# Spreading the top-16 steps and gate writes of a PEER layer, with an early norm, a bias spread in DRAM and a new tail

## The chip, the cores and the metric

The kernel runs on one core of a Trainium2 chip. The metric is the device time of one execution in microseconds (us), the median over runs. A core has five engines that run their instruction streams in order and side by side: TensorE (PE, matmul, with its weight load as PEld), VectorE (DVE), ScalarE (ACT), GpSimd (POOL) and SyncE (SP). SP issues most DMAs, POOL the others. Sixteen DMA engines move the data of all queues.

## The reference

One layer of a decoder with batch 1, 256 tokens (T) and width 2048 (D), all in fp32:

```python
h = h + concat(nsa(rmsnorm(h)), stick_breaking(rmsnorm(h))) @ w_out
h = h + memory_attention(rmsnorm(h), rmsnorm(mem))
h = h + peer_ffn(rmsnorm(h))
return rmsnorm(h, norm_final)
```

The change touches three places of it. In the NSA attention a T5 bias, which depends only on the distance of query and key, is added to the logits of 8 heads. In PEER each of 8 heads projects a token to two queries of 128, scores each against 128 sub-keys, takes the 16 best of both, then the 16 best of their 256 sums, and so chooses 16 of 16384 experts:

```python
q = (xt @ w_pq).reshape(T, 8, 2, 128)
s = jnp.einsum('thpd,hpkd->thpk', q, sub_keys)
top_s, top_i = lax.top_k(s, 16)
cand = top_s[:, :, 0, :, None] + top_s[:, :, 1, None, :]
best_s, best_c = lax.top_k(cand.reshape(T, 8, 256), 16)
expert = ia * 128 + ib                     # of the two winners
gate = jax.nn.softmax(best_s, axis=-1)
a = jnp.einsum('td,ted->te', xb, u_tab[eb])
out = jnp.einsum('te,ted->td', gate * jax.nn.gelu(a), v_tab[eb])
```

The last place is the closing rmsnorm over the 256 x 2048 result.

## The kernel before

Every fp32 weight tile of 128 x 1024 ("raw", 512 KB, loaded by SP) is split for TensorE: ACT copies it to `hi` (L72), DVE forms the rest `lo` = raw - hi (L74). `fm_block` multiplies two such halves: per half eight matmuls of `hi` with the pair of the activations' high and low parts (L109) and eight of `lo` with the high part (L111). `join` adds the two parts of the result (ACT L144, DVE L145). There are 4 buffers of raw and 3 each of hi and lo.

The stages in order: attention over memory and tokens with its projections, up to about 547 us, of which `bias_table` prepares the T5 bias; PEER's queries, 16 blocks of `w_pq` (8 heads h, two queries p2 each); 128 blocks of U (`u_chunk`), one for each 128 experts, which hold for all tokens the gelu of their dot products; then V.

The block h = 7, p2 = 1 is `whole_block`: raw fp32 matmuls (L138) with `whole`, the unsplit activations. `whole` is put together on POOL from the two parts of `x3` (L712). After it `renew` multiplies `whole` by the tokens' `rstd` (L795, in place) and splits it anew into `x3` (L796, L797) for the U blocks, which so work on normed tokens; the `w_pq` blocks before work on tokens without `rstd`, which `keys` puts into the scores (L934).

The top-16 is cut into 48 pieces: for each head and half of the tokens (tb) `keys` (scores on PE L932, 16 best of each side), `pairs` (best 16 of 256 sums, softmax) and a third (`ids` and `sums`: expert numbers, `place` as a table index, and for experts that an earlier head chose too, the sum of the gates with `dup`, L989 to L995, growing with the head). Nearly all of it is DVE work on 16 to 256 (at the end 1792) elements a partition. `topk_pieces` returns the three functions, the loop calls one a block.

A gate goes to a table in DRAM by `put_gate` (L1016): an indirect DMA on POOL writing 128 words of 4 bytes, 256 of them (128 for each tb). `some` issues the next few, each `behind` a recent `lo` (a wait on the last or last but one `lo` issued, so POOL goes in step with the blocks). Later the table is read back (L810), multiplied with the gelu values, the hit tokens of each expert are counted and listed (`lists`), rows are written (L904) and V rows are fetched (L1067). In the V phase `run(0)` to `run(3)` go over lists of experts by halves; `steps` are functions that it calls between the halves, one every second turn; `closing` then forms the final rmsnorm for both halves of the tokens from the eight accumulators in PSUM, and stores it.

The program's order on each engine is set by a scheduler that simulates the program and honours data dependencies, buffers and added dependencies (`add_manual_dep`). `SYNC` as its kind is a wait on the chip; the change adds a kind `NoSync`, which only fixes an order within an engine.

Of the kernel before, what the change touches and what calls it, by code (L numbers as in the profile page):

```python
# [22 lines left out]
SYNC = mybir.DependencyInfo(mybir.DependencyClass.Sync, mybir.DependencyReason.DATA)  # L23
AF = mybir.ActivationFunctionType
# [3 lines left out]
T = 256  # L28
# [24 lines left out]
class Layer:  # L53
    def __init__(self, tc, a):
        self.tc, self.nc, self.a = tc, tc.nc, a
        self.written = ([], [])
        self.spread = {}
        self.pace = []

# [9 lines left out]
    def parts(self, raw, eng=None):  # L69
# [5 lines left out]
        self.pace.append(self.last_lo)  # L75
        return hi, lo
# [20 lines left out]
    def scaled(self, raw, val):  # L97
# [4 lines left out]
        self.last_lo = nc.vector.scalar_tensor_tensor(lo, raw, val, hi.bitcast(F32), op0=ALU.mult, op1=ALU.subtract)  # L102
        return hi, lo

# [75 lines left out]
    def rsqrt(self, v, y, tmp):  # L180
# [7 lines left out]
        nc.vector.tensor_mul(y, y, tmp)  # L188
# [53 lines left out]
    def front(self):  # L242
        nc, tc, a = self.nc, self.tc, self.a
        with ExitStack() as es:
# [52 lines left out]
            turned = self.bias_table()  # L297
# [23 lines left out]
            turned()  # L321
# [113 lines left out]
    def bias_table(self):  # L435
# [10 lines left out]
        row = fp.tile([8, 512], F32, tag="p", name="row", bufs=2)  # L446
        nc.vector.tensor_add(row, p, neg)

        dr = self.dram.tile([8, 512], F32, name="bias_rows")
        nc.gpsimd.dma_start(dr, row)  # L450
# [4 lines left out]
        turn = fp.tile([128, 128], F32, tag="tri", name="turn")  # L455
        nc.gpsimd.dma_start(turn, a["turn"])
# [4 lines left out]
        def turned():  # L461
            for tb in range(2):
                for h in range(0, 8, 2):
                    p = self.ps.tile([128, 2, T], F32, tag="lg", name="ps_turn", bufs=2)
                    nc.tensor.matmul(p, turn, rev[:, tb, h:h + 2, :], start=True, stop=True)
                    nc.scalar.activation(self.bias[:, tb, h:h + 2, :], p, AF.Copy)

        return turned
# [202 lines left out]
    def peer(self):  # L671
        nc, tc, a = self.nc, self.tc, self.a
        with ExitStack() as es:
# [13 lines left out]
            def some(todo=puts, n=3):  # L687

                if not n:
                    n = 3 + beat[0] % 2  # L690
                    beat[0] += 1
# [4 lines left out]
            with ExitStack() as e2:  # L696
                ps = self.ps = e2.enter_context(tc.tile_pool(name="ups", bufs=2, reuse_waits="tile", space=bass.MemoryType.PSUM))
                pieces = []
                with tc.tile_pool(name="tk", bufs=1, reuse_waits="tile") as tk:
                    self.tk = tk  # L700
                    self.gate = [tk.tile([128, 128], F32, name="gate%d" % tb) for tb in range(2)]
                    self.spot = [tk.tile([128, 128], F32, name="spot%d" % tb) for tb in range(2)]
# [6 lines left out]
                    for q in range(4):  # L709
                        xs = slice(q * 4, q * 4 + 4)  # L710
                        x32 = self.x3[:, xs, :].bitcast(F32)
                        nc.gpsimd.tensor_add(whole[:, xs, :], x32[:, :, :T], x32[:, :, T:])  # L712
                    for h in range(8):
                        sk = tk.tile([128, 2, 128], F32, tag="sk", name="sk", bufs=2)
# [5 lines left out]
                        for p2 in range(2):  # L720
                            q = tk.tile([128, T], F32, tag="q", name="q", bufs=4)
# [30 lines left out]
                end = c + (len(puts) + 2) // 3  # L752
# [5 lines left out]
                while c < 128:  # L758
# [8 lines left out]
                    self.u_chunk(c, c >= first)  # L767
                    for g, t in done.pop(c, []):
# [3 lines left out]
                    some()  # L772
# [11 lines left out]
                    if not steps:  # L784
                        some(late)
# [4 lines left out]
    def renew(self, whole):  # L790
        nc = self.nc
        for q in range(4):
            xs = slice(q * 4, q * 4 + 4)
            src = whole[:, xs, :]
            nc.vector.tensor_tensor(out=src, in0=src, in1=self.rstd.unsqueeze(1).to_broadcast([128, 4, T]), op=ALU.mult)  # L795
# [610 lines left out]
```

## Time and profile before

| | |
|---|---|
| median of 3 runs | 1749.74 us (1748.86 to 1755.26) |
| profiled execution | 1753.41 us |
| its span, first to last instruction | 1751.4 us |
| mean granted TensorE clock | 0.977 |
| PE busy | 1656.6 us, 95% |
| DVE busy | 1248.1 us, 71% |
| ACT busy | 984.6 us, 56% |
| POOL busy | 743.7 us, 42% |
| DMA | 414.93 MB, mean 237 GB/s |

The page of the profile divides the span into 40 equal slices and gives the busy share of each engine in tenths, and the clock that TensorE was granted. Other views give busy times by stretches of time, groups of instructions by line and operation ("xcount | busy us, mean ns | idle time before, and what ended it"), waits ("engine line waited for: us in total, times, longest"), and the chain of work that ended last, followed back from the end. "remote" or "another core or an unknown queue" there stands for a semaphore whose writer the profile doesn't show. Matmuls overlap, so their mean durations add up to more than the busy time.

### The profile page before, as it was taken

To read this page: it belongs to the slowest core of one execution; us is meant where nothing else is said; L and a number is where in the kernel's file an instruction comes from. 1 tells how busy PE (TensorE), PEld (TensorE's weight loads), DVE (VectorE), ACT (ScalarE), POOL (GpSimd) and SP (SyncE) were. 2 spreads that over 40 slices of the span, in tenths; PEclk is the share of its full clock that TensorE was granted. 3 is DMA by queue.
4 is the path that set the end of the run, shared out by engine and by line. 5 is a ranking of instruction groups with operands and counts; after the bars stand their busy time and mean duration, and the time that the engine had idled before them with its cause. 6 is when DMAs were issued, how large, how long until landed. Compare 5 with 4: busy or idle time off the path is not lost.

```text
span 1751.4 us, 25883 instructions
## 1 busy us (share of the span) xinstructions
PE 1656.6 (95%) x8864; PEld 1400.7 (80%) x8864; DVE 1248.1 (71%) x2231; ACT 984.6 (56%) x1457; POOL 743.7 (42%) x652
## 2 busy tenths in 40 slices
PE   8999999999999786999999999999999988999996
PEld 6788777888888675888888888888888776777885
DVE  6835475556659789999994557886666568788687
ACT  6534556765565333665654446664555446666566
POOL 5510000112217444787886551103655307786620
PEclk9999999999999888999999999999999999999998
DMA  8656435789946543565666657886888965998991
GB/s 295 228 171 209 143 104 193 275 318 362 333 143 189 173 124 104 175 193 173 199 193 176 189 180 258 283 281 220 262 258 262 351 252 202 415 385 332 412 399 61
DMA packets 136475, 414.93 MB, mean 237 GB/s; under 512 B 39177, under 2 KB 52105, under 8 KB 122768
## 3 DMA queue, kind: packets, MB, share of 16 engines
q1 hardware_dynamic: 97712, 254.21, 45.4%
q0 software_dynamic: 38624, 158.99, 24.0%
q8 instruction: 71, 1.16, 0.3%
q14 instruction: 68, 0.56, 0.1%
HBM read 369.26 MB, written 49.65 MB: 239 GB/s over the span
## 4 chain that ended last, share of the span: by engine, by line
PE 54%; DVE 7%; DMA 5%; issue 4%; ACT 2%; POOL 1%; another core or an unknown queue 1%; POOLq 0%; ACTq 0%; DVEq 0%
PE acc L109 28%; PE acc L111 14%; PE out L1095 11%; DMA raw<-U 2%; DVE lo L74 2%; DMA vrows<-V,index 1%; ACT hi L72 1%; DVE pair_f L177 1%; DMA gates<-table 1%; POOL rows L904 1%; DMA rows<-hb,where 1%; POOL vrows L1067 0%; PE out L1197 0%; PE ps_s L932 0%
## 5 line engine op out<-in xcount | busy, mean ns | idle before, releaser
L74 DVE TENSOR_TENSOR lo<-raw,hi 128x1024 fp32r<-128x1024 f32 x433 | 535.4, 1240 | 303.8 <-ACT hi L72 210.7
L72 ACT ACTIVATE hi<-raw 128x1024 fp32r<-128x1024 f32 x437 | 461.1, 1058 | 452.5 <-issue 161.3
L109 PE MATMUL acc<-pair_f,hi 128*128 128x512 f32 x2288 | 580.8, 396 | 17.2 <-ACT hi L72 7.4
L109 PEld LDWEIGHTS acc<-pair_f,hi 128*128 128x128 f32 x2288 | 415.9, 191 | 96.4 <-ACT hi L72 8.3
L1016 POOL DMA_INDIRECT table<-total,place x256 | 308.6, 1206 | 177.3 <-DVE lo L74 69.6
L111 PEld LDWEIGHTS acc<-pair_f,lo 128*128 128x128 f32 x2288 | 314.1, 192 | 23.6 <-DVE lo L74 1.6
L111 PE MATMUL acc<-pair_f,lo 128*128 128x256 f32 x2288 | 322.3, 284 | 1.4 <-issue 0.8
L904 POOL DMA_INDIRECT rows<-hb,where x128 | 153.8, 1201 | 123.3 <-DVE lo L74 76.2
L102 DVE SCALAR_TENSOR_TENSOR lo<-vrows,val,hi 128x1024 fp32r<-128x1024 f32 x96 | 122.7, 1284 | 42.4 <-ACT hi L100 33.2
L100 ACT ACTIVATE hi<-vrows,val 128x1024 fp32r<-128x1024 f32 x96 | 109.0, 1147 | 78.1 <-PE out L1095 36.2
L1067 POOL DMA_INDIRECT vrows<-V,index x88 | 116.6, 1325 | 65.4 <-issue 19.2
L109 PE MATMUL acc<-pair_x,hi 128*128 128x512 f32 x512 | 131.9, 396 | 0.0
L74 DVE TENSOR_TENSOR lo<-vrows,hi 128x1024 fp32r<-128x1024 f32 x80 | 97.8, 1223 | 16.0 <-ACT hi L72 6.6
L109 PEld LDWEIGHTS acc<-pair_x,hi 128*128 128x128 f32 x512 | 91.7, 189 | 17.2 <-issue 1.4
L72 ACT ACTIVATE hi<-vrows 128x1024 fp32r<-128x1024 f32 x80 | 84.2, 1052 | 26.5 <-PE out L1095 20.9
L1095 PE MATMUL out<-hi,hh 128*128 128x512 f32 x256 | 79.7, 405 | 4.5 <-DVE ut L145 2.3
L1095 PE MATMUL out<-hi,hl 128*128 128x512 f32 x256 | 81.5, 403 | 1.0 <-DVE hl L1104 0.4
L1095 PE MATMUL out<-lo,hh 128*128 128x512 f32 x256 | 76.7, 402 | 0.2 <-DVE lo L74 0.2
L111 PEld LDWEIGHTS acc<-pair_x,lo 128*128 128x128 f32 x512 | 71.1, 192 | 5.2
L111 PE MATMUL acc<-pair_x,lo 128*128 128x256 f32 x512 | 75.1, 286 | 0.0
L109 PE MATMUL acc<-pair_o,hi 128*128 128x512 f32 x256 | 65.0, 394 | 5.7 <-ACT hi L72 4.7
L1095 PE MATMUL out<-hi,listed 128*128 128x512 f32 x192 | 59.7, 402 | 5.0 <-ACT hi L100 4.5
(393 smaller groups left out, 2209.4 us busy)
## 6 DMA issues: line engine op xcount, KB each, us to landing
raw<-U SPq DMA_DIRECT2D x256, 512.0 KB
raw<-w_sb SPq DMA_DIRECT2D x32, 512.0 KB
table<-zero POOLq DMA_DIRECT2D x16, 1024.0 KB
raw<-w_out SPq DMA_DIRECT2D x32, 512.0 KB
raw<-w_pq SPq DMA_DIRECT2D x32, 512.0 KB
listed<-rows SPq DMA_DIRECT2D x88, 129.0 KB
rows<-zero POOLq DMA_DIRECT2D x12, 903.0 KB
gates<-table POOLq DMA_DIRECT2D x20, 512.0 KB
```

The source lines that it names most:

```text
L72: nc.scalar.activation(hi, raw, AF.Copy)
L74: self.last_lo = (eng or nc.vector).tensor_tensor(out=lo, in0=raw, in1=hi.bitcast(F32), op=ALU.subtract)
L100: nc.scalar.activation(hi, raw, AF.Copy, scale=val)
L102: self.last_lo = nc.vector.scalar_tensor_tensor(lo, raw, val, hi.bitcast(F32), op0=ALU.mult, op1=ALU.subtract)
L109: mm(ps, hi[:, n * m:(n + 1) * m], pair[:, k, :], start=first and n == 0, stop=False)
L111: mm(ps[:, T:], lo[:, n * m:(n + 1) * m], pair[:, k, :T], start=False, stop=last and n == len(ks) - 1)
L177: nc.vector.scalar_tensor_tensor(pair[:, k, T:], src, g, pair[:, k, :T].bitcast(F32), op0=ALU.mult, op1=ALU.subtract)
L904: ins = nc.gpsimd.indirect_dma_start(out=self.rows[part], out_offset=bass.IndirectOffsetOnAxis(ap=where[:, i - lo:i - lo + 1], axis=0), in ...
L1016: ins = self.nc.gpsimd.indirect_dma_start(out=self.table, out_offset=bass.IndirectOffsetOnAxis(ap=self.place[tb][:, s:s + 1], axis=0), in_ ...
L1067: nc.gpsimd.indirect_dma_start(out=raw, out_offset=None, in_=self.a["V"], in_offset=bass.IndirectOffsetOnAxis(ap=self.index[part, cls][:, ...
L1095: mm(out[tb][hf * 2 + q], h, v[:, q * 512:(q + 1) * 512], start=first and n == 0, stop=last and n == len(passes) - 1)
```

## The change

1. **Top-16 steps.** `sk` gets 8 buffers in place of 2, `q` 16 in place of 4. The first DVE instruction of each piece is ordered (not waited for) behind the last `lo` issued. Pieces are taken in blocks b with b % 5 != 4, over both the `w_pq` blocks and the U blocks (b = 2 to 61; before, one in every block from 2 to 49). `place` is written directly as integers, without `spot` and its cast (L979).
2. **Gate writes.** They begin in block 9 and go 3 and 4 a block in turn up to the end; before they began as soon as the first stood in the list, and went 3 a block after the last piece. The later row writes also go 3 and 4 a block in turn (before 3).
3. **Normed tokens early.** `whole` is loaded from the copy of the residual in DRAM (`hres`), scaled on ACT by the gain and on POOL by `rstd`, ahead of the query blocks. `renew` only splits it. The last query is then normed already, so `keys` leaves its `rstd` out.
4. **Bias.** The 8 rows of 512 are spread to 128 copies in DRAM, and two DMAs read the bias from it along a diagonal, behind the last `lo` of the `w_q` blocks. The reversed read, 16 matmuls (L465) and 8 ACT copies (L466) go.
5. **Tail.** The first half's closing runs as steps between the halves of `run(3)`, one each turn. The last products are ordered by bank. The second half closes after them, its work over ACT and DVE, its stores over two queues. `held` keeps a later `lo` from being ordered between the steps of the root.

```diff
+ORDER = mybir.DependencyInfo(mybir.DependencyClass.NoSync, mybir.DependencyReason.DATA)
...
+    def held(self):
+        if self.hold is not None:
+            self.tc.add_manual_dep(self.last_lo.ins, self.hold.ins.name, ORDER, reason="not between the steps of a root")
+            self.hold = None
...
-        rev = fp.tile([128, 2, 8, T], F32, tag="pair", name="rev")
-        for tb in range(2):
-            src = bass.AP(tensor=dr.tensor, offset=dr.offset + 128 - tb * 128, ap=[[1, 128], [512, 8], [1, T]])
-            nc.gpsimd.dma_start(rev[:, tb], src)
...
+        dr = self.dram.tile([128, 8, 512], F32, name="bias_rows")
+        nc.gpsimd.dma_start(dr, one.unsqueeze(0).to_broadcast([128, 8, 512]))
...
+        def spread():
             for tb in range(2):
-                for h in range(0, 8, 2):
-                    p = self.ps.tile([128, 2, T], F32, tag="lg", name="ps_turn", bufs=2)
-                    nc.tensor.matmul(p, turn, rev[:, tb, h:h + 2, :], start=True, stop=True)
-                    nc.scalar.activation(self.bias[:, tb, h:h + 2, :], p, AF.Copy)
+                src = bass.AP(tensor=dr.tensor, offset=dr.offset + 255 - tb * 128,
+                              ap=[[8 * 512 - 1, 128], [512, 8], [1, T]])
+                self.behind(nc.gpsimd.dma_start(self.bias[:, tb], src), 1)
...
+                def step(b):
+                    if pieces and b % 5 != 4:
+                        pieces.pop(0)()
+                    if b >= 9:
+                        some(n=0)
...
-                        nc.gpsimd.tensor_add(whole[:, xs, :], x32[:, :, :T], x32[:, :, T:])
+                        nc.gpsimd.dma_start(whole[:, xs, :], self.hres[:, xs, :])
+                        for k in range(q * 4, q * 4 + 4):
+                            nc.scalar.activation(whole[:, k, :], whole[:, k, :], AF.Copy, scale=self.gs[:, 3, k:k + 1])
+                        nc.gpsimd.tensor_tensor(out=whole[:, xs, :], in0=whole[:, xs, :],
+                                                in1=self.rstd.unsqueeze(1).to_broadcast([128, 4, T]), op=ALU.mult)
...
-                        sk = tk.tile([128, 2, 128], F32, tag="sk", name="sk", bufs=2)
+                        sk = tk.tile([128, 2, 128], F32, tag="sk", name="sk", bufs=8)
...
-                            q = tk.tile([128, T], F32, tag="q", name="q", bufs=4)
+                            q = tk.tile([128, T], F32, tag="q", name="q", bufs=16)
...
-                            if pieces:
-                                pieces.pop(0)()
-                            some(n=0)
+                            step(2 * h + p2)
...
-                        pieces.pop(0)()
-                        some(n=0)
+                        step(16 + c)
...
-                end = c + (len(puts) + 2) // 3
+                end = c + (2 * len(puts) + 6) // 7 + 1
...
-                        some(late)
+                        some(late, 0)
...
-            nc.vector.tensor_tensor(out=src, in0=src, in1=self.rstd.unsqueeze(1).to_broadcast([128, 4, T]), op=ALU.mult)
...
+        def pin(ins):
+            self.tc.add_manual_dep(ins.ins, self.last_lo.ins.name, ORDER, reason="beside its block")
...
-            nc.vector.tensor_scalar(self.spot[tb][:, hs], key[:, 0], float(T), self.token[:, tb:tb + 1],
+            nc.vector.tensor_scalar(self.place[tb][:, hs], key[:, 0], float(T), self.token[:, tb:tb + 1],
                                     op0=ALU.mult, op1=ALU.add)
-            nc.vector.tensor_copy(self.place[tb][:, hs], self.spot[tb][:, hs])
...
+                for n, q in sorted(order, key=lambda x: x[1]) if last else order:
...
+            run(3, steps=[lambda: None] + head(out[0]), every=1)
+            closing(out[1])
```

More of the change, by code (lines that the diff above doesn't have):

```diff
@@ L687, in some @@
             def some(todo=puts, n=3):
-                if not n:
+                if not n and todo:
                     n = 3 + beat[0] % 2
@@ L933, in keys @@
             st["s"] = w([128, 2, 128], "s")
-            nc.scalar.activation(st["s"], p, AF.Copy, scale=self.rstd_c[:, tb:tb + 1])
+            for n in range(2):
+                if h == 7 and n == 1:
+                    nc.scalar.activation(st["s"][:, n, :], p[:, n, :], AF.Copy)
+                elif h == 7 or n == 0:
+                    ns = slice(0, 1 if h == 7 else 2)
+                    nc.scalar.activation(st["s"][:, ns, :], p[:, ns, :], AF.Copy, scale=self.rstd_c[:, tb:tb + 1])
             st["v"] = w([128, 2, 16], "v")
@@ L1092, in products @@
                 first = not started[tb][hf]
-                for n, (h, v) in enumerate(passes):
-                    for q in range(2):
-                        mm(out[tb][hf * 2 + q], h, v[:, q * 512:(q + 1) * 512], start=first and n == 0,
-                           stop=last and n == len(passes) - 1)
+                order = [(n, q) for n in range(len(passes)) for q in range(2)]
+                for n, q in sorted(order, key=lambda x: x[1]) if last else order:
+                    h, v = passes[n]
+                    mm(out[tb][hf * 2 + q], h, v[:, q * 512:(q + 1) * 512], start=first and n == 0,
+                       stop=last and n == len(passes) - 1)
                 started[tb][hf] = True
@@ new lines, in rest, with scale, head, whole_root @@
+                def rest():
+                    self.hold = self.rsqrt(v, y, t)
+                return y, mean, rest
+            def scale(src, y, q):
+                og = fin[:, 3, cut(q)]
+                nc.scalar.activation(og, src[q], AF.Copy, scale=y)
+                nc.gpsimd.tensor_mul(og, og, gain[:, cut(q)])
+                nc.sync.dma_start(a["out"][:128, cut(q)], og)
+            def head(src):
+                z = sums("z0")
+                y, mean, rest = root(z)
+                def whole_root():
+                    mean()
+                    rest()
+                return ([lambda: square(0, src, z, 0), lambda: square(0, src, z, 1), lambda: square(0, src, z, 2),
+                         lambda: square(0, src, z, 3), whole_root, lambda: None]
+                        + [(lambda q=q: scale(src, y, q)) for q in range(4)])
@@ L1226, in closing @@
             def closing(src):
-                z = squares(src[0])
-                og = fin[:, 3, :]
+                z = sums("z1")
+                og = [fin[:, 0, cut(q)] for q in range(4)]
+                y, mean, rest = root(z)
                 for q in range(4):
-                    cs = slice(q * 512, (q + 1) * 512)
-                    nc.vector.tensor_mul(og[:, cs], src[0][q], gain[:, cs])
-                y = root(z)
+                    square(1, src, z, q)
+                    nc.vector.tensor_mul(og[q], src[q], gain[:, cut(q)])
@@ L1265, in again @@
                         nc.vector.tensor_add(whole[tb][q], whole[tb][q], out[tb][q])
-                closing(whole)
+                for step in head(whole[0]):
+                    step()
+                closing(whole[1])
             self.rest(hidden_pair, products, reopen, again)
```

94 lines of the change are left out of this document (40 added, 54 removed).

## The prediction

> **What bounds the kernel now.** I read the page's slices of the span first, then the busy time by stretches, the waits of the worst stretch, and the chain of work that ended last there.
>
> ```profile
> PE   8999999999999786999999999999999988999996
> PEclk9999999999999888999999999999999999999998
> ```
>
> Slices of 43.8 us. TensorE is the bound nearly everywhere; the one wide hole is slices 14 to 16 (569 to 700 us), where the queries of PEER are projected and the top-16 begins, and the granted clock falls there too. Next the stretches (PE, PEld, DVE, ACT, POOL busy with counts, granted clock, DMA share, GB/s):
>
> ```profile
> 553.00:600.00 47.00, 46.85 (x279) 41.41 (x278) 43.83 (x114) 21.91 (x31) 26.48 (x18) 1.00 0.69 190
> 600.00:625.00 25.00, 6.65 (x30) 5.72 (x29) 8.40 (x34) 5.41 (x9) 14.32 (x15) 0.59 0.25 74
> 625.00:700.00 75.00, 60.00 (x299) 50.73 (x298) 73.62 (x258) 28.45 (x46) 34.05 (x29) 0.89 0.39 120
> 700.00:920.00 220.00, 220.00 (x1268) 193.94 (x1267) 208.88 (x497) 135.24 (x199) 172.53 (x128) 1.00 0.62 187
> ```
>
> From 700 to 920 PE has no gap although DVE is busy 208.88 of 220 (95%): that is the state to compare with. From 553 to 700 PE idles 0.15 + 18.35 + 15.00 = 33.5 us. Its busy time at a lower clock costs a further 6.65 x 0.41 + 60.00 x 0.11 = 9.3 us. **So at most 42.8 us can be won in this stage.**
>
> The hole has two causes. The first, by the waits of 575 to 625 and the chain there:
>
> ```profile
> POOL table L1016 <- DVE place L979: 17.9, 1, 17.9
> PE ps_s L932 <- ACT s L934: 17.5, 1, 17.5
> ACT hi L72 <- remote: 11.8, 1, 11.8
> DVE lo L74 <- remote: 10.1, 1, 10.1
> ```
> ```profile
> 596.40 4.09 issue
> 600.55 12.77 another core or an unknown queue
> 614.40 4.01 another core or an unknown queue
> ```
> ```profile
> 595.00:600.00 5.00, 5.00 (x34) 4.55 (x33) 4.99 (x15) 1.35 (x3) 4.09 (x4) 1.00 0.65 202
> 610.00:615.00 5.00, 0.00 (x0) 0.00 (x0) 0.00 (x0) 1.06 (x1) 3.82 (x4) 0.50 0.08 24
> L1016 POOL DMA_INDIRECT table<-total,place x21: 978/980/1567, 588.0 to 615.0; - x21
> L1016 POOL DMA_INDIRECT table<-total,place x126 | 170.5, 1353 | 47.4 <-issue 32.2 <-DVE ab L962 3.3 <-DVE lo L74 3.1
> ```
>
> POOL had waited 17.9 us for the first places; by then the pacing waits of the queued gate writes were long met, and it issued 21 of them (third row) back to back, one each (615.0 - 588.0) / 20 = 1.35 us. Meanwhile ACT and DVE waited for something the profile doesn't name, on weights loaded by DMA, with the DMA engines 8% busy and PE still. Work comes back as the burst ends. Between 700 and 916 the same writes (fourth row: 126) were 216 / 126 = 1.71 us apart, and PE lost nothing. I read the burst as the cause; that it is no coincidence isn't shown.
>
> The second, from 625 to 700, by the waits there:
>
> ```profile
> PE acc L109 <- DVE pair_f L797: 6.0, 3, 2.7
> PE acc L138 <- issue: 4.1, 1, 4.1
> ```
> ```profile
> L795 DVE TENSOR_TENSOR whole<-whole,rstd x4: 1222/1226/1226, 668.7 to 677.5; 128x1024 f32<-128x1024 f32 x4
> ```
>
> DVE is full (73.62 of 75) and in order. Four buffers of `q` and two of `sk` force the top-16 of the early heads through before the next projections, and `renew` multiplies `whole` in place, which it can only do once the raw matmuls L138 have read it.
>
> **The change part by part.**
>
> *Gate writes from block 9, 3 and 4 a block.* The first places come from the third piece of head 0, now in block 5, so POOL no longer waits for them and then hurries. The 17.5 us wait and its slow clock go. What is late next is DVE. Spread over 4 blocks of 5, top-16 takes blocks 2 to 61. A block of a steady stretch:
>
> ```profile
> 624.86 1.84 PE acc L109 x8
> 626.70 0.95 PE acc L111 x8
> 692.74 3.04 PE acc L109 x8
> ```
> ```profile
> L138 PE MATMUL acc<-whole,raw 128*128 128x256 f32 x32 | 10.1, 493 | 4.1 <-issue 4.1
> ```
>
> A half is 1.84 + 0.95 = 2.79 us, a block 5.58 (third row: the same eight after idling take 3.04, the price of the lower clock). The raw block's 32 matmuls of 493 ns (overlapping, so 10.1 busy) take 15.8, 10 more than a block.
>
> DVE's load in the new order: 43.83 + 8.40 + 73.62 + 208.88 = 334.7 us were done from 553 to 920. The change takes off four multiplies (4.9) and sixteen casts of `place` (about 16 x 0.2, from the row below), leaving 326.6; and five more blocks of `lo` and join fall into the same span: before, (367 - 43 lost - 10 extra of the raw block) / 5.58 = 56 blocks ran in it, and top-16 is now to end with the 61st after 553. At two `lo` of 1.2 us and a join of 0.4 these add 5 x 2.9 = 14.5. That is 341 us in 61 x 5.58 + 10 = 350: 97%, against 95% where PE lost nothing. Within it the load rises:
>
> ```profile
> L979 DVE CAST place<-spot x16: 150/164/464, 587.5 to 905.3; 128x16 uint32<-128x16 f32 x16
> L989 DVE TENSOR_TENSOR dup<-spot x14: 414/1218/2019, 644.6 to 905.4; 128x256 f32<-128x256 f32 x2, 128x512 f32<-128x512 f32 x2, 128x768 f32<-128x768 f32 x2, 128x1024 f32<-128x1024 f32 x2
> ```
>
> Three operations like L989 grow from 0.4 to 2.0 us with the head, 3.2 us on average over the 16 sets (head, half). Of the 334.7 us, 56 x 2.9 are `lo` and joins, 10 `renew` and by my estimate 6 other work; 156 are left for 16 sets, 9.7 each, 6.5 without those three. So a set of head 7 asks 10.9 (`lo`, joins) + 6.5 + 3 x 2.0 = 23.4 us in 3.75 blocks of 5.58 = 20.9, and heads 5 to 7 together are over by about 9 us. The pins hold a piece from running early, not from running late, so `lo` can go first and pieces trail, as they trailed before. I charge **+2**, of 0 to 9.
>
> *Buffers, pins and normed tokens.* The eight `sk`, sixteen `q` and the early norm take away the reasons of the second hole. `whole` costs 4 loads, 16 ACT scales and 4 POOL multiplies; the last take the place of four additions:
>
> ```profile
> L712 POOL TENSOR_TENSOR whole<-pair_f x4: 2396/3092/3456, 557.7 to 566.1; 128x1024 f32<-128x1024 f32 x4
> L144 ACT ACTIVATE q<-acc 128x256 f32<-128x256 f32 x4 | 1.5, 367 | 0.0
> ```
>
> 16 x 0.37 = 6 us on ACT, which is busy 21.91 of 47 there; needed some 80 us later. Nothing, unless ACT stands in order behind a late load: 0 to +6. Of the 42.8 us I leave the 4.1 at L138 (no wait named) and 2 for clock and rounding: **-37**, bounds -15 (second hole alone, burst unchanged) and -42.8.
>
> *The rest of the gate writes.* They cost 1353 ns each beside a busy DVE; with the issue time 32.2 / 126 between them, 3.5 x 1.61 = 5.6 us a block, against 5.58: POOL stays full and trails. It did before, and when top-16 ended it caught up:
>
> ```profile
> L1016 POOL DMA_INDIRECT table<-total,place x13: 977/980/1471, 915.9 to 933.1; - x13
> 914.00:934.00 20.00, 17.86 (x99) 15.11 (x98) 8.39 (x10) 5.83 (x9) 15.05 (x15) 0.99 0.75 163
> 934.00:940.00 6.00, 6.00 (x28) 5.26 (x29) 3.92 (x4) 4.56 (x7) 2.56 (x3) 0.74 0.46 139
> ```
>
> 2.14 idle and 6 x 0.26 + 0.2 of clock = 3.9 us for 13 writes in a row. After the change the same can come at block 62: **-1**, of -3.9 to +4. The Trainium skill, "SBUF — State Buffer", section "SBUF: two separate sides", says that GpSimd can't write the descriptors of its DMAs while certain DVE operations hold a shared port. The trace agrees in part: 1353 ns beside the DVE of 700 to 916, but 980 at the median in the burst. By it, more writes beside top-16 mean a slower POOL; it speaks against this part, and is rival 3.
>
> *Bias spread in DRAM.*
>
> ```profile
> 100.00:225.00 125.00, 125.00 (x698) 103.12 (x696) 55.31 (x84) 55.41 (x94) 2.06 (x3) 1.00 0.54 174
> L465 PE MATMUL ps_turn<-rev,turn 128*128 128x512 f32 x16 | 8.1, 617 | 0.0
> 174.40 1.23 DVE L74 TENSOR_TENSOR lo<-raw,hi 128x1024 fp32r<-128x1024 f32 x1 [1.56 <-ACT hi L72]
> 204.51 0.48 DVE L568 SCALAR_TENSOR_TENSOR l<-ps_l,qscale,bias 128x256 f32<-128x256 f32 x1
> q0 software_dynamic: 546, 2.10, 33.6%
> ```
>
> PE has no gap here, so its 16 matmuls are on the path: **-8**. The two diagonal reads wait for a `lo` that ends by 175.6, 28.9 us ahead of first use; the two reads of `rev`, as large, moved inside 62 to 80 us (last row: 2.10 MB in 18). The broadcast of 2 MB has over 90 us. What queues behind the waiting reads on POOL is little: it is busy 2.06 of 125 us there. Bounds: -8.1, and 0 if the reads come 8 us late.
>
> *Tail.*
>
> ```profile
> 1735.52 0.74 PE L1095 MATMUL out<-lo,listed 128*128 128x512 f32 x2
> 1739.47 0.19 ACT L1210 ACTIVATION_READ_ACCUMULATOR sq<-out 128x1 f32 x1
> 1741.95 2.07 DVE L1249 SCALAR_TENSOR_TENSOR fin<-out,fy,fin 128x512 f32<-128x512 f32 x3
> 1700.00:1736.00 36.00, 36.00 (x156) 28.44 (x154) 33.89 (x45) 28.76 (x35) 0.00 (x0) 1.00 0.23 83
> ```
>
> From the last matmul (1736.26) to the last scale (1744.02) are 7.8 us. After: one square left (0.8), the root 1741.95 - 1739.66 = 2.3, two scales an engine (1.3): 4.4, so -3.4. The first half's closing, some 6 us of ACT and 2 of DVE, moves into the last stretch, where ACT has 7.2 us free and DVE 2.1: it may hold the last `lo` up a little. **-2.5**, of -4 to +2.
>
> Sum: -37 + 2 - 1 - 8 - 2.5 = -46.5. The profiled execution took 1753.41 us (span 1751.4 and 2.0 around it), 3.7 above the median of 1749.74. From the median: **1703**.
>
> **The rivals.**
>
> 1. *DVE becomes the bound.* The pins keep pieces behind their blocks, and where they stand ahead of the next `lo`, PE waits: 9 us in heads 5 to 7, as much again if early blocks are no better packed, 2 of it charged already. For it: 97%. Against: 95% cost nothing. 1703 + 16 = 1719.
> 2. *The burst wasn't the cause*, and the 21 us of 600 to 625 stay (18.35 and 2.7 of clock), whatever the unnamed queue waited for. For it: the idle DMA engines, which a mere crowd of 21 small writes doesn't explain. The Trainium skill, "DMA: Bandwidth & Descriptors", section "Queues, rings and completion order", has each engine take turns between rings by packet, by which loads would pass such writes; no row here shows the turns. Against: the hole begins and ends with the burst, and 13 in a row cost PE 3.9 again. 1703 + 21 = 1724; with rival 1, 1740.
> 3. *Slower:* POOL, full at 5.6 us a block of 5.58, never keeps the pace. Each time DVE's `lo` or a place is late, the writes behind it lose their spacing and come as a burst again. A burst of 21 costs 21 us; it decides from the third, which takes more than the gain of 46.5: 1703 + 63 = 1766. For it: both bursts of before came when POOL had waited or trailed. Against: 126 writes of a full POOL from 700 to 916 cost PE nothing.
> 4. *The holes belong to the profiled execution alone.* It is 3.7 us above the median, so at most that much of the 42.8 is its own: 1707, inside the forecast's range and with no chance apart.
>
> **How the numbers follow.** Forecast (1686 to 1713) 0.60; rival 1 (1719) 0.12; rival 2 (1724) 0.14; both (1740) 0.07; rival 3 (1766) 0.07. The ends of the likeliest case: all bounds well, -42.8 - 3.9 - 8.1 - 4 = -58.8, 1691, and 5 below for losses I haven't counted; badly, 7 more of DVE and 3 more of the tail or the last burst. The range 1686 to 1728 takes in rivals 1 and 2. Half a per cent (8.7 us) is about what a measurement of this kernel can tell from no change: faster holds the first three, 0.86; same 0.07 (the fourth, on the edge of it); slower 0.07.
>
> **What would show it.** Right: the stretch from 553 to 700 has PE at 97% or more and clock 1.00, no wait "remote" over 3 us, gate writes 1.4 to 1.8 us apart from about 600 on, no wait for `pair_f`; nothing of L465 and V's last matmul some 45 us earlier; under 5 us from it to the last scale. Wrong: PE waiting for `lo` while DVE is full (rival 1), a wait "remote" of 10 us with or without a burst (rivals 3, 2), or L568 waiting for a DMA.

## The result, and the profile after

The changed kernel takes 1726.28 us (median of 5 runs, 1722.91 to 1735.1) against 1750.37 of the kernel before (1748.86 to 1755.26). The ratio is 0.9869, with a 95% interval of 0.9837 to 0.99. It is faster by 24 us; 46.5 were forecast. The profiled execution took 1726.28 us; its span is 1724.5 us, 26.9 shorter than that of before.

The slices of the page of the changed kernel (43.1 us each):

```profile
PE   8899999999999999999999899989999888999996
PEclk9999999999999999999999899999999989999998
```

The wide hole in slices 14 to 16 is gone. New dents of PE stand in the 23rd and the 27th slice, and the clock dips in the 23rd and the 33rd. The four stretches of before again (PE, PEld, DVE, ACT, POOL busy with counts, granted clock, DMA share, GB/s):

```profile
553.00:600.00 47.00, 42.84 (x239) 37.18 (x238) 42.60 (x112) 26.93 (x49) 14.67 (x9) 0.96 0.77 229
600.00:625.00 25.00, 25.00 (x145) 21.98 (x145) 22.71 (x62) 11.06 (x15) 17.90 (x16) 1.00 0.64 189
625.00:700.00 75.00, 75.00 (x430) 66.16 (x429) 66.48 (x180) 45.08 (x66) 58.93 (x47) 1.00 0.60 185
700.00:920.00 220.00, 218.96 (x1266) 192.77 (x1265) 208.43 (x534) 137.66 (x203) 171.03 (x129) 1.00 0.62 183
```

From 600 to 700 PE has no gap and a full clock, where it idled 33 us before. From 553 to 600 it has one that it did not have: 4.2 us. So the stage did nearly what was forecast. To see where the rest went, the trace was read by halves of blocks. Each half of a `w_pq` or U block is eight matmuls of `hi` and eight of `lo`, and a steady one starts 2.793 us after the one before. What a start is later than that is a loss (other matmuls of PE in between count as one too). Summed by stretches, in us, for both profiled executions, and for a second pair of them from a later group of runs (described below):

| stretch | before | changed | before, 2nd | changed, 2nd |
|---|---|---|---|---|
| first `w_pq` block starts at | 546.9 | 540.8 | 548.4 | 541.5 |
| loss in `w_pq` blocks 0 to 4 | 1.3 | 1.3 | 1.3 | 1.3 |
| blocks 4 to 6 (halves 9 to 12) | 0.4 | 7.0 | 0.5 | 6.1 |
| blocks 6 to 14 | 25.9 | 0.5 | 9.8 | 0.5 |
| raw block to U block 1 (6.7 are the raw block) | 29.8 | 7.3 | 30.5 | 7.3 |
| U blocks 2 to 39 | 0.7 | 5.0 | 0.7 | 3.6 |
| U blocks 40 to 58 | 5.4 | 12.0 | 1.0 | 1.5 |
| U blocks 59 to 84 | 3.5 | 0.1 | 5.9 | 0.0 |
| U blocks 85 to 94 (lists) | 8.9 | 16.3 | 9.0 | 16.7 |
| U blocks 95 to 127 | 6.8 | 8.8 | 6.4 | 5.2 |
| last `hi` matmul of U to the last 96 V products | 286.3 | 288.0 | 284.5 | 289.2 |
| last 96 V products to the end of the span | 37.8 | 39.9 | 37.8 | 39.5 |

At U block 54 the changed kernel was 47 us ahead of before, as much as the whole forecast. Then it lost 10 us in three blocks, 7 at the lists, and 4 in V and at the end.

**The new stall in the 23rd slice.** Two stretches of it, its waits, and the gate writes (L1040 in the changed kernel; count, and duration in ns as least, median, greatest):

```profile
955.00:960.00 5.00, 2.01 (x7) 1.18 (x6) 1.60 (x2) 0.39 (x1) 3.78 (x5) 0.84 0.80 263
960.00:965.00 5.00, 2.70 (x7) 1.48 (x5) 0.00 (x0) 1.36 (x2) 2.09 (x3) 0.50 0.05 10
```
```profile
DVE lo L76 <- remote: 7.5, 1, 7.5
ACT hi L74 <- remote: 6.7, 1, 6.7
```
```profile
L1040 POOL DMA_INDIRECT table<-total,place x11: 967/968/987, 949.0 to 961.7; - x11
```

It has the signature of the stall that before had at 600 us: gate writes back to back (11 in 12.7 us, 1.27 each), ACT and DVE waiting for something that the profile calls remote, idle DMA engines (0.05), half the clock. It came when top-16 ended, DVE went quiet, and POOL caught up.

**What the remote waits are for.** The prediction put them down to weights that DMA had still to load. The times of the semaphore updates in the trace (a semaphore is the counter by which one engine tells another that an instruction is done) say otherwise. In the kernel before, the `hi` that starts at 613.34 and the `lo` that starts at 618.38 need the load that SP issued at 593.8, and the last packet of all loads issued up to 599.2 is done at 602.7. What ends their waits is PE's own semaphore: updates of it are recorded at 606.2, 613.3 and 618.3 to 618.5, though PE's last instruction that sends one ended at 601.4 by the trace. The latest of these updates so come 17.0 us late. SP in the meantime issues little: its longest wait is for the same semaphore, and so the DMA engines idle (start, duration and issues of SP, and that wait):

```profile
587.64 20.18 SPq L63 DMA_DIRECT2D raw<-w_pq  x6
618.47 0.33 SPq L715 DMA_DIRECT2D sk<-subkeys  x1
SPq L715 <- remote: 10.6, 1, 10.6
```

In the stall of the changed kernel ACT goes on at 962.4, on an update of PE's semaphore at 962.33 that comes 6.7 us after the last instruction that sends one. Before the last 20 us of the span, DVE's and ACT's updates are never more than 0.03 us late, in any trace. Whether PE's matmuls ended late or only their signal can't be told, since the ends of matmuls are modelled.

**The new loss at blocks 4 to 6.** The timeline of POOL and DVE there (start, duration, engine, line, operation):

```profile
563.69 11.44 POOL L726 TENSOR_TENSOR whole<-whole,rstd 128x1024 f32<-128x1024 f32 x4 [9.61 <-DVE rstd L198]
```
```profile
567.29 2.31 DVE L966 TENSOR_TENSOR cand<-v 128x256 f32<-128x256 f32 x1
569.53 3.36 DVE L76 TENSOR_TENSOR lo<-raw,hi 128x1024 fp32r<-128x1024 f32 x1
572.81 2.35 DVE L982 CAST if<-i 128x32 f32<-128x32 uint32 x1
```

While POOL multiplies `whole` by `rstd`, three DVE operations take 2.31, 3.36 and 2.35 us, which elsewhere take 0.4, 1.2 and 0.2. The Trainium skill, "SBUF — State Buffer", section "SBUF: two separate sides", describes this: one port pair is shared by DVE and GpSimd, held for a whole instruction, and the other engine waits. The trace agrees: three of POOL's multiplies end at 569.3, 571.8 and 575.1, and the three DVE operations 0.3, 1.1 and less than 0.1 us behind them.

**The end.** The same two engines in the last stretch of V, and what PE waits for:

```profile
1702.38 8.73 POOL L1255 TENSOR_TENSOR fin<-fin 128x512 f32<-128x512 f32 x4 [40.84 <-ACT fin L1254]
```
```profile
1703.20 2.32 DVE L76 TENSOR_TENSOR lo<-vrows,hi 128x1024 fp32r<-128x1024 f32 x1
1705.44 2.31 DVE L105 SCALAR_TENSOR_TENSOR lo<-vrows,val,hi 128x1024 fp32r<-128x1024 f32 x1
1707.67 2.29 DVE L76 TENSOR_TENSOR lo<-vrows,hi 128x1024 fp32r<-128x1024 f32 x1
1709.89 2.31 DVE L105 SCALAR_TENSOR_TENSOR lo<-vrows,val,hi 128x1024 fp32r<-128x1024 f32 x1
```
```profile
1710.02 0.73 PE L1120 MATMUL out<-lo,hh 128*128 128x512 f32 x2 [1.48 <-DVE lo L76]
1712.25 0.78 PE L1120 MATMUL out<-lo,listed 128*128 128x512 f32 x2 [1.03 <-DVE lo L105]
```
```profile
1716.29 1.33 ACT L1280 ACTIVATE fin<-fin,fy 128x512 f32<-128x512 f32 x2 [1.00 <-DVE fy L198]
```

POOL's four multiplies of the first half's closing stretch each `lo` from 1.25 to 2.3 us. The last 96 products take 28.0 us instead of 22.3. The end behind them did shrink as forecast: ACT's part of the last scales (two from 1716.29 on, last row) ends at 1717.6, 4.6 us after PE at 1713.0, and the span's remainder from the start of the last product went from 15.5 to 11.9 us. Net the new tail costs 2.1 us.

### The profile page after: what moved, and what is told of

Its sections match the earlier page's. It is cut to its first block, busy times and chain, and to the rows that moved or that the text cites. A ratio compares the mean times of both kernels' runs of the same rounds, so it can differ in the third digit from the quotient of the medians.

```text
span 1724.5 us, 25797 instructions
## 1 busy us (share of the span) xinstructions
PE 1647.3 (96%) x8848; PEld 1393.5 (81%) x8848; DVE 1249.7 (72%) x2208; ACT 995.1 (58%) x1476; POOL 775.2 (45%) x659
## 5 line engine op out<-in xcount | busy, mean ns | idle before, releaser
L1040 POOL DMA_INDIRECT table<-total,place x256 | 324.3, 1267 | 124.9 <-issue 62.8
L915 POOL DMA_INDIRECT rows<-hb,where x128 | 163.6, 1278 | 61.1 <-issue 36.3
L76 DVE TENSOR_TENSOR lo<-vrows,hi 128x1024 fp32r<-128x1024 f32 x80 | 99.8, 1248 | 12.7 <-issue 4.8
```

Of the source, the lines that this page charges most:

```text
L76: self.last_lo = (eng or nc.vector).tensor_tensor(out=lo, in0=raw, in1=hi.bitcast(F32), op=ALU.subtract)
L915: ins = nc.gpsimd.indirect_dma_start(out=self.rows[part], out_offset=bass.IndirectOffsetOnAxis(ap=where[:, i - lo:i - lo + 1], axis=0), in ...
L1040: ins = self.nc.gpsimd.indirect_dma_start(out=self.table, out_offset=bass.IndirectOffsetOnAxis(ap=self.place[tb][:, s:s + 1], axis=0), in_ ...
```

## The experiments

Times differ between groups of runs: the kernel before took 1750 to 1752 us in some groups and 1730 to 1732 in others. A time is therefore set against before in the same group, and a loss against traces of groups alike. The losses are those of the table.

The two kinds of group differ in their traces too. In all ten traces of groups with before at 1750 some of PE's semaphore updates come late, by 2.7 to 17.0 us at the most, and none by more than 1 us until the gate writes have begun. In the nine traces of the other groups none is more than 0.02 us late before the last 20 us of the span. The ten also lack 7 to 15% of the updates of PE, DVE and ACT, the nine at most 0.3%.

### Three repairs and the gate writes' pace (group with before at 1752.19)

**x1, no POOL in the first half's closing.**

```diff
-                nc.scalar.activation(og, src[q], AF.Copy, scale=y)
-                nc.gpsimd.tensor_mul(og, og, gain[:, cut(q)])
+                nc.vector.scalar_tensor_tensor(og, src[q], y, gain[:, cut(q)], op0=ALU.mult, op1=ALU.mult)
```

> The changed kernel with one thing else: the four scales of the first half's closing are one DVE operation each (times root, times gain) instead of an ACT scale and a POOL multiply. Theory (POOL's multiplies block DVE's operations that read two SBUF tiles): the last lo operations take 1.25 us again instead of 2.3, PE's waits of 1.2 to 1.5 us in the last five pairs go, about 1726 to 1721 us. Rival (DVE is merely full at the end): four more DVE operations of 0.7 us make it no better, 1726 to 1729.

1729.22 us (1718.24 to 1736.49), ratio 0.9876 (0.9833 to 0.9918). The timeline of DVE and of PE in it:

```profile
1696.77 2.72 DVE L1254 SCALAR_TENSOR_TENSOR fin<-out,fy,fin 128x512 f32<-128x512 f32 x4
1699.41 1.21 DVE L76 TENSOR_TENSOR lo<-vrows,hi 128x1024 fp32r<-128x1024 f32 x1
```
```profile
1700.68 0.88 PE L1120 MATMUL out<-lo,hh 128*128 128x512 f32 x2 [0.85 <-DVE lo L76]
```

`lo` takes 1.21 us again, so the port theory holds for the durations. But the last 96 products still take 26.8 us (28.0 in the changed kernel, 22.3 before), and with the end 38.3 (39.9 and 37.8): the four scales stand in a row on DVE for 2.72 us, and `lo` comes late behind them. The rival holds for the time: DVE has nothing to give there, whether it is blocked or given work.

**x2, `whole` normed on DVE.** The POOL multiply goes, and one quarter at a time is done on DVE, pinned behind the last `lo` of blocks 4, 9, 10 and 14.

```diff
-                        nc.gpsimd.tensor_tensor(out=whole[:, xs, :], in0=whole[:, xs, :],
-                                                in1=self.rstd.unsqueeze(1).to_broadcast([128, 4, T]), op=ALU.mult)
...
                             step(2 * h + p2)
+                            if 2 * h + p2 in (4, 9, 10, 14):
+                                norm.pop(0)()
```

> The changed kernel with the four multiplies of whole by rstd on DVE, one each in blocks 4, 9, 10 and 14, instead of four on POOL of about 3 us each beside blocks 3 to 5. Theory (the POOL multiplies block DVE there): DVE operations between 563 and 575 us take their usual times (lo 1.2 instead of 3.4, the cast 0.2 instead of 2.4), and the 7 us that PE lost in blocks 4 and 5 go, about 1726 to 1720 us. Rival (ACT stands in order behind the 16 scales and their loads, or the sub-key and number loads stand ahead of the weights): the loss stays at 5 to 7 us and the time at 1726.

1728.81 us (1723.07 to 1732.06), ratio 0.9853 (0.981 to 0.9896). The loss in blocks 4 to 6 is 6.1 us, hardly less than 7.0. DVE's operations there take their usual times, but the longest wait of 560 to 582 us is now another:

```profile
566.49 0.41 DVE L974 TENSOR_TENSOR cand<-v 128x256 f32<-128x256 f32 x1
566.81 1.22 DVE L76 TENSOR_TENSOR lo<-raw,hi 128x1024 fp32r<-128x1024 f32 x1
569.08 0.17 DVE L990 CAST if<-i 128x32 f32<-128x32 uint32 x1
```
```profile
ACT hi L74 <- DMA raw<-w_pq: 8.0, 2, 6.0
```

The weights are late. In the changed kernel 8 loads of sub-keys (2 before) and 8 of expert numbers stand among them on SP, and 12.6 us pass between two weight loads (552.2 to 564.8; before at most 7.5). DVE's blocked operations had covered that.

**x3, the later eight loads of numbers spread.**

```diff
-                for b in range(8):
-                    self.hidden_tile(bb)
...
                 while c < 128:
+                    while len(self.buf) < 16 and c >= 8 * len(self.buf) - 14:
+                        self.hidden_tile(bb)
```

> The changed kernel with the eight loads of expert numbers (8 KB each in pieces of 8 bytes), which stood together after the top-16, given one every eight U blocks instead. Theory A (these loads of some 9000 small packets hold the weights up): the stall of PE at 955 to 967 us (10 us and a clock of 0.5) goes, 1726 to about 1716. Theory B (gate writes back to back hold them up): the stall stays, 1726.

1728.93 us, ratio 0.986 (0.9821 to 0.9898). It didn't do what it was meant to: SP, which nothing held, still issued all eight from 946 to 956 us. The loss in U blocks 40 to 58 was 10.0 us. So it decides nothing.

**x4, 3 gate writes a block, then 4.**

```diff
                     if b >= 9:
-                        some(n=0)
+                        some(n=3)
...
-                end = c + (2 * len(puts) + 6) // 7 + 1
+                end = c + (len(puts) + 3) // 4
...
-                    some(n=0)
+                    some(n=4)
```

> The changed kernel with 3 gate writes a block up to the last top-16 step and 4 a block after, instead of 3 and 4 in turn. Theory B (POOL falls behind at 3.5 writes of 1.6 us a block and catches up back to back when DVE goes quiet, which stalls the weights): POOL keeps the pace, no stretch of more than 8 writes at 1.27 us, no stall at 955, 1726 to about 1717. Theory A (the loads of numbers): the stall stays, 1726.

1728.93 us, ratio 0.9864 (0.9828 to 0.9901). POOL didn't keep the pace: 12 writes from 966.4 to 981.8 stand 1.40 us apart, and its closest six 1.33 (1.27 in the changed kernel). In U blocks 40 to 58 it lost 6.9 us instead of 12.0, but 11.2 instead of 0.1 in U blocks 59 to 84. Of these, 5.0 lie where the writes at 4 a block ran, up to 1046 us, and 6.2 behind the last of them. So what was gained at one place was lost at others; that the writes caused either part isn't shown.

### The old tail, the loads' pace, and the burst (group with before at 1732.08)

**y1, the tail of before** (part 5 of the change undone), one run.

> The changed kernel with the tail of before (first half's closing after the last V products, products in the old order). Theory (the steps put into the last stretch cost more than the shorter end saves, since DVE had no time to give there): from the last U block to the end 325 to 326 us as before, against 329.5 with the new tail, so 3 to 4 us faster. Rival (V is longer for another reason, the earlier V fetches): 329 to 331 us, the new tail's shorter end being lost.

1714.18 us. The last 96 products and the end take 38.7 us, of which the products 22.3 as before; 39.9 and 39.5 in the changed kernel's two traces. The new tail costs 1 to 2 us, not 3 to 4: from the last half of U to the end it took 331 us, the rival's number, and the front part of V is what varied.

**y2, the loads of sub-keys and numbers paced,** one run:

```diff
-                        nc.sync.dma_start(sk, a["subkeys"][:, 2 * h:2 * h + 2, :])
+                        self.behind(nc.sync.dma_start(sk, a["subkeys"][:, 2 * h:2 * h + 2, :]), 4)
```

and the same for the loads of numbers, with x3's spreading.

> The changed kernel with each load of sub-keys and of expert numbers made to wait for the fourth last lo, and the second eight loads of numbers given one every eight U blocks. In blocks 4 to 6 (7.0 us lost): if these loads stand ahead of the weights, the loss falls to 0 to 3; if POOL's multiplies are enough to cause it, it stays at 4 to 7. At 950 to 965 us (10.5 us lost): if the loads of numbers cause it, 0 to 2; if the gate writes alone, 8 to 10; if both are needed, 3 to 5.

1709.71 us. In blocks 4 to 6 it still lost 5.6 us, and DVE's operations were blocked as in the changed kernel. So neither cause is enough to be taken away alone. At 950 to 965 nothing was lost, but nothing was lost there in any kernel of this group, so the loads of numbers aren't convicted by it.

**x5, 24 gate writes given at once in block 9,** one run:

```diff
-                    if b >= 9:
+                    if b == 9:
+                        some(n=24)
+                    elif b >= 16:
                         some(n=0)
```

> The changed kernel with 24 gate writes given at once in block 9, and then none before block 16, 3 and 4 a block from there. Theory (gate writes back to back hold the weights up): a stall of PE of 10 to 25 us within 15 us of about 600 us, with waits that the profile calls remote. Rival (the stall of before at 600 us had another cause): under 3 us lost there.

1710.33 us, and 0.5 us lost in blocks 6 to 14: no stall. The rival's number came; but beside the busy DVE these writes came 1.27 to 2.2 us apart, and the group is one in which before itself hardly stalls, as its second trace showed next.

**z1 and z4, the kernel before with only the gate writes begun later.**

```diff
-                            some(n=0)
+                            if 2 * h + p2 >= 9:
+                                some(n=0)
...
-                end = c + (len(puts) + 2) // 3
+                end = c + (2 * len(puts) + 6) // 7
...
-                    some()
+                    some(n=0)
```

> The kernel before with one part of the change: gate writes from block 9 on, 3 and 4 a block to the end. Theory (the burst of 21 caused the stall at 600): the 21 us of 596 to 621 go and the second hole from 650 to 690 stays, 1750 to about 1728 us. Rival (the stall has another cause): it stays, 1750.

> The kernel before with gate writes from block 9 on, a second time. In a group where before takes 1750: theory (the burst causes the stall) 1728 to 1735 us and under 11 us lost in halves 13 to 29 instead of 26; rival (another cause) 1750 and 20 us or more. In a group where before takes 1731: 1735 to 1742 as the first time, which tells nothing new.

1740.11 us against 1732.08, ratio 1.0051 (1.0034 to 1.0069), and in another group 1737.4 against 1730.59, ratio 1.005 (1.0026 to 1.0073): slower, by half a per cent. In both the loss in blocks 6 to 14 was 9.9 us, as in the second trace of before (9.8). So in such a group the burst costs nothing that the losses show, and this part alone brings nothing. z4 itself has a longer stretch of writes back to back, and PE has no gap in it:

```profile
L1017 POOL DMA_INDIRECT table<-total,place x38: 978/1064/1221, 919.2 to 970.9; - x38
919.00:972.00 53.00, 53.00 (x305) 46.67 (x304) 27.53 (x31) 26.30 (x40) 41.41 (x38) 1.00 0.71 203
```

Whether it would have taken the 21 us away where before takes 1750 wasn't seen, since both groups were of the other kind.

### The same two kernels again, and a joint version (group with before at 1730.15)

> The kernel before, unchanged, for a second trace: in the last group of runs it took 1732 us instead of 1750. If the stall at 596 to 621 us is a fixed property of its order, it is there again with about 21 us; if it comes and goes with the chip's circumstances, a run of about 1732 us has under 5 us there, and one of about 1750 has it.

> The changed kernel, unchanged, in the same circumstances as the kernel before. If the stalls beside gate writes come and go with the circumstances: in a group where before takes 1732 us this one takes about 1711, with no loss at 950 to 965 us; where before takes 1750, about 1727 with a loss of some 10 us there.

The kernel before took 1735.37 us in its profiled run, the changed one 1713.94 (1705.16 to 1716.17), ratio 0.9883 (0.983 to 0.9936). Both are faster than in the first group, the profiled runs by 18 and 14 us, and the table shows where: before lost 9.8 us instead of 25.9 in blocks 6 to 14, the changed kernel 1.5 instead of 12.0 in U blocks 40 to 58. (The changed kernel's profiled run has a span of 1709.9 us.) The writes of before in this trace, and the stretch:

```profile
L1016 POOL DMA_INDIRECT table<-total,place x20: 978/981/1842, 589.5 to 615.8; - x20
600.00:625.00 25.00, 22.72 (x126) 19.74 (x125) 24.07 (x88) 10.60 (x17) 19.51 (x19) 0.93 0.60 172
```

20 writes, (615.8 - 589.5) / 19 = 1.38 us apart (1.35 in the first trace), and PE busy 22.72 of 25 us instead of 6.65. The same burst of the same program went with a stall of 21 us in one group. In the other the half of a block at 598 us lost 4.8 us, and it loses 4.6 in z1 and z4, whose writes begin at 602.

**y5, reads two U blocks earlier,** one run:

```diff
-                end = c + (2 * len(puts) + 6) // 7 + 1
+                end = c + 20
...
-                    some(n=0)
+                    some(n=4)
```

> The changed kernel with 4 gate writes a block after the last top-16 step and the early table reads from U block 66 on, as before, instead of 68. Theory (the move by two blocks puts the counting of hits and the lists' first matmuls beside a table read): from U block 85 to 95 the loss beyond PE's steady pace falls from 16 us to the 9 us of before. Rival (the loss is another's, or of chance): 14 us or more.

1715.99 us. The loss at the lists is 8.9 us, just that of before: the theory holds. But U blocks 59 to 84 now lost 14.3 us. The wait that stands for it, from 1005 to 1025:

```profile
DVE hb L783 <- DMA gates<-table: 14.1, 2, 12.9
```

The first reads of the table wait for the last gate writes, and DVE, in order, waits for the reads with the `lo` behind them. The later reads avoid that and pay at the lists: about a draw.

**c1, together:** x2, y2 and y5, and a third tail, in which only the first half's four squares run beside V and all the rest comes after.

> The changed kernel with all that should help: the multiplies of whole on DVE, the loads of sub-keys and numbers paced, the first half's squares alone in the last V stretch and the rest of both closings after it, reads two U blocks earlier. Theory: the loss in blocks 4 to 6 falls from 6 or 7 us to under 2 (it has two causes and both are gone), the last V stretch with the end from 40 to about 36 us, the lists' loss to 9: 15 us below the changed kernel in the same group. Rival (each cause was covered by the next): under 6 us below.

1704.91 us (1703.42 to 1708.05), ratio 0.984 (0.98 to 0.988), 9.0 us below the changed kernel in the same group, where 15 were expected (the runs of the two touch: up to 1708.05 here, from 1705.16 there). In blocks 4 to 6 it lost 0.0 us: with both causes gone the loss is gone. The last 96 products and the end take 37.9 us (39.5), the lists 9.5, the reads' start 12.3.

### Parts alone, and the reads again (group with before at 1752.24)

**z2, the kernel before with 8 and 16 buffers** (`sk`, `q`), and **z3, with the early norm** (part 3), one run each:

> The kernel before with one part of the change: 8 buffers of sub-keys and 16 of queries. Theory (too few buffers force the top-16 of early heads ahead of the projections, which fills DVE): of the second hole (halves 29 to 34, 30 us beyond PE's pace, of which 7 are the raw block itself) 10 us or more go. Rival (renew's wait for the raw matmuls is the hole): under 5 us go.

> The kernel before with one part of the change: whole loaded, scaled and normed early, renew only splitting it. Theory (renew's wait is a smaller part): 5 to 10 us of the second hole go. Rival (it is the whole hole): 18 us or more go. POOL's multiplies beside the first top-16 steps may cost up to 7 us at 565 to 575.

z2 took 1740.6 us, z3 1750.7. Of the second hole (29.8 us), z2 leaves 12.6 and z3 20.7, 6.7 of both being the raw block: 17 us go with the buffers, 9 with the norm, and both theories hold. z3 also lost 6.2 us in blocks 4 to 6, as the changed kernel did. z2 shows the bursts again. Twelve of its writes, and PE in a stretch with them:

```profile
L1016 POOL DMA_INDIRECT table<-total,place x12: 979/981/983, 608.3 to 622.4; - x12
608.00:626.00 18.00, 9.13 (x25) 5.32 (x25) 5.45 (x25) 1.70 (x3) 11.78 (x12) 0.63 0.20 60
```

14.7 us were lost there, and 10 at another burst of 14 writes at 828 to 844, where neither a load of numbers nor the start of top-16 stands near.

**c2 and c3, the joint version with the reads as in the change, and one U block earlier.**

> All amendments of the joint version but the earlier reads: loss at the lists 16 us, none at the reads' start, against 9.5 and 12 in the joint version; the V stretch up to its last 96 products 288 us instead of 283, if V's start is held by something that does not move with the U blocks. Sum: 1705, within 3 us of the joint version; clearly better (1699) only if V keeps its 283.

> The joint version with the early reads one U block later than in it. Theory (they waited there for the last gate writes, POOL being behind): the 8 us lost at the reads' start fall to under 4, the lists' loss stays 9 to 10, 1700 us. Rival (any offset but two is bad for the lists, or the loss at the start is the reads' own): 1705 or more.

1720.14 us, ratio 0.9817 (0.9792 to 0.9842), and 1718.06, ratio 0.9796 (0.9767 to 0.9825). c2 came by its parts: 16.9 us lost at the lists, 1.6 at the reads' start, 290.6 us of V up to the last 96 products, and a ratio that doesn't differ from the joint version's beyond the intervals. c3 missed: at the reads' start it lost 10.3 us, at the lists 14.2, and only V was short (281.6). In c3 the loads of numbers were spread at last (936, 968, 1017 us and later), and 18 gate writes stood back to back from 937 to 959 us: 14.4 us lost there, 5.4 in c2 with gaps between its writes. So the loss goes with the writes and not with the loads of numbers. By their ratios all three joint versions (0.984, 0.9817, 0.9796) stand ahead of the changed kernel (0.9869 and 0.9883); only c1 was run in one group with it.

## Why the prediction was wrong, by its own steps

- **What bounds the kernel, and the second hole: right.** It was put down to the buffers and to `renew`; z2 and z3 divide it into 17 and 9 us, which overlap a little. The raw block costs 1.1 us more than a block (6.7 against 5.6), not the 10 that were read by adding up its matmuls, which overlap and ran in part at the low clock.
- **The stage from 553 to 700, -37 and +2 for DVE: right in size, by errors that cancel.** The losses up to U block 39 fell by 57.4 - 16.1 - 4.3 = 37 us. But the two holes gave 25.4 + 22.5 = 47.9 (about 3 of it score matmuls that moved to later blocks), more than the 42.8 that were called the most; `whole` (next point) and the U blocks 2 to 39 took the rest back. The 4.3 of these blocks are in the main not DVE's: 40 score matmuls stand there instead of 16, which came from the blocks before, at about 0.11 us each. From 700 to 920 PE idles 1.0 us (218.96 of 220 busy) with DVE at 95%, and in the second trace not at all. So DVE was priced too high, not too low.
- **Whole's cost "nothing, unless ACT stands in order behind a late load: 0 to +6": wrong in value and in cause.** 7.0 us, from POOL's multiplies holding up DVE and from loads ahead of the weights on SP; each alone costs 6 (x2, y2), both away 0 (c1). The step that failed is the price of POOL's four multiplies: they were set equal to the four additions of before, beside which PE lost next to nothing, and what DVE does beside them was not looked at.
- **"The rest of the gate writes, -1, of -3.9 to +4": the step that failed most.** +6.6 us. POOL did trail, and did catch up back to back at the end of top-16, as the step says; a burst of 11 was priced by one of 13 in the trace of before (3.9 us) and went with a loss of 10. The price of a burst isn't fixed: in the second pair this term is +0.5. Rival 3's mechanism took place once, not three times.
- **The first burst as the cause, and rival 2:** "on weights loaded by DMA" was misread: the weights had landed, and the wait was for PE's semaphore, up to 17.0 us late. In groups with before at 1750 the large losses of this kind, 4 to 21 us, all stand at a stretch of 11 or more writes back to back (before twice, z2 twice, z3, the changed kernel, x2, c3), though not each such stretch has one (x2: 12 writes 1.38 us apart from 972 to 987, no loss). In the other groups a stretch of 38 costs nothing. So the burst alone isn't the cause: in one kind of group it goes with late updates, in the other not. That it is needed there is likely, since nearly all late updates stand beside dense writes, but z1 and z4, which take it away, met no such group. Of the 25.9 us of blocks 6 to 14, 9.8 are lost without such a stall too, and 16 were a gain of the first group only; in the other the changed kernel is still faster by 16 us of median.
- **Bias, -8: 6.2 us at the first `w_pq` block** in one pair of traces and 6.9 in the other, inside the bounds.
- **Tail, -2.5, of -4 to +2: wrong, +2.1.** The 3.4 us at the end came (15.5 - 11.9 = 3.6). The "2 of DVE" that move into the last stretch were not all: POOL's multiplies took DVE's time as well, and DVE had 2.1 us to spare. The section of the Trainium skill that the prediction named for the gate writes, "SBUF: two separate sides" of "SBUF — State Buffer", has the rule quoted above, and it was not applied to POOL's arithmetic.
- **Left out of the sum:** the lists (+7.4 us), since the reads move by two U blocks. The prediction looked at no stage beyond the writes.

From the table, by stages: -6.2 (bias), -37 (stage), +6.6 (writes), +6.0 (U blocks 59 to 127), +3.8 (V and tail) are the 26.9 us of the spans. In the second pair they are -6.9, -24.0, +0.5, +0.6 and +6.4, the 23.5 us of its spans. The totals are close by luck: in the one there was a stall of 16 us to win back and a new one to pay, in the other neither.

What stays open is why PE's updates come late beside the same burst in some groups and not in others. It isn't the chip: groups of both kinds ran on the same one. The Trainium skill, "DMA: Bandwidth & Descriptors", section "Queues, rings and completion order", has each DMA engine alternate between rings by packet; by that the loads would not be held up. The trace of before agrees: the load issued at 599.2 landed within 3.5 us, beside the burst.

## What to carry to other kernels

When work goes to GpSimd because it looks free, ask what DVE does at that moment: a tensor operation there doubled DVE's, and at the end of a stage where DVE has no slack it came straight out of PE's time. Where an engine waits for something that the profile calls remote, look up the semaphore before a queue is blamed: here it was PE's. Pace a stream of small writes over the whole stretch in which they are made and beyond: where they catch up, they catch up as a burst, and a burst went with a stall in half of the groups here. A loss with two causes shows no gain when one is removed; remove both before the theory is dropped.

## What was not expected of the hardware

Beside a burst of small indirect writes, 1.27 to 1.35 us apart, semaphore updates of TensorE came up to 17.0 us late, so that ACT, DVE and SP stood with the weights loaded and the DMA engines 5 to 8% busy. The same burst of the same program did no such thing in another group of runs (PE busy 6.65 and 22.72 of 25 us). A one-input cast of 128x32 elements took 2.35 us beside a GpSimd multiply and 0.17 without it, as long a wait as that of DVE's operations with two inputs.
